# Expert stage of a streaming encoder: stores on another queue, seven key groups taken straight through, float32 gate products, one selection at a time

## The chip, the core and the metric

The program runs on one core of one Trainium2 chip. The metric is the device time of one execution in microseconds, and the number that is compared is the median over several runs.

## The reference, cut to what is computed

One encoder layer runs over 256 prompt tokens and 128 sample tokens of width 2048. The change touches the last but one part of the layer, a product-key retrieval over 128 x 128 = 16384 one-neuron experts (PEER):

```python
def one_block(xt):
    q = (xt @ wq).reshape(blk, PEER_HEADS, 2, PEER_DKEY // 2)
    s = jnp.einsum('thpd,hpnd->thpn', q, keys).astype(jnp.float32)
    sv, si = lax.top_k(s, PEER_TOPK)
    cand = (sv[..., 0, :, None] + sv[..., 1, None, :]).reshape(blk, PEER_HEADS, PEER_TOPK * PEER_TOPK)
    ...
    top_v, top_p = lax.top_k(cand, PEER_TOPK)
    e_idx = jnp.take_along_axis(cidx, top_p, -1).reshape(blk, PEER_HEADS * PEER_TOPK)
    gate = jax.nn.softmax(top_v, -1).reshape(blk, PEER_HEADS * PEER_TOPK)
    act = jax.nn.gelu(jnp.einsum('ted,td->te', u_tab[e_idx], xt).astype(jnp.float32))
    coef = (gate * act).astype(xt.dtype)
    return jnp.einsum('te,ted->td', coef, v_tab[e_idx])
```

Before it come the token mixers, after it a layer norm and a gated embedding product. All weights are float32.

## The kernel before, in words

**Two ways through the experts.** The 128 sample tokens fetch their own experts: 256 gathers of 1 MB each (`fetch_experts`, L1420; 128 rows of `u_rows`, then 128 of `v_rows`), issued on GpSimd (L1426) and each used by one VectorE instruction (L1433 for a dot product, L1440 for a weighted sum into `xg`). The 256 prompt tokens go dense: the first product of all 16384 experts with all tokens, times a gate matrix that is zero where a token did not choose the expert, times the second table. This dense way is cut into 256 units of work on TensorE, each with one weight tile `st` of 1 MB (128x2048 f32) and 48 matmuls of 256 columns: 128 units of the first product (`u_unit`, one per row of keys) and 128 of the second (`v_unit`, 16 key groups of 8 rows times 8 slices of the width).

**A weight tile.** Class `Units` loads it on SP's queue (L104, three buffers), ScalarE rounds each half to a high part `wh` (L118), VectorE or GpSimd subtracts for the low part `wl` (L121), with four buffers each of half a tile. Each matmul triple is high x high, high x low, low x high. `lo_on_pool` says how many of the two halves GpSimd takes: during the first products of a tile with an odd number 2, otherwise 1.

**The order.** It is written by hand. A counter advances by one tick per matmul triple, so a unit has 16 ticks; every 15 ticks a gather step is emitted (`GEVERY`; the instruction that uses a gathered tile follows `LAG` = 3 steps behind, `NGB` = 5 tiles), and other work is a generator that is resumed every so many ticks (`start(..., every)`). In the last query projections the sample tokens' selection (`select_fetched`) runs so; the program then empties the list of generators (`drain_to(0)`) before the first unit.

**The dense gates.** `matrices` is one such generator. For each of the two tiles of 128 prompt tokens it runs `select` (top 16 of 128 twice per head, top 16 of 256 sums, indices and softmax on VectorE) and `turn` (transposes on TensorE into the PSUM tile `pe` and into `eT`), both tiles' selections first, every 7 ticks; then `gates_matrix` for both tiles, every 4 ticks. It goes by steps of 4 tokens, 32 per tile, 16 ticks each. In a step VectorE builds one-hot tiles `AB` (L1405), ScalarE scales the first key's one-hots by the high and the low part of the gates (`H`, eight instructions, L1414), TensorE multiplies them in four float32r matmuls of 256 columns into the single PSUM tile `pg` (twice two), and after each two ScalarE copies the high part to `GB` (L1392) and VectorE adds the low part (L1393). Every 8 steps SP stores `GB` (2 MB) to the DRAM tensor `G_dr` (L1395).

**Between the products.** The GELU of every pair of first products is stored by SP to `act_dr` (L1469), 64 stores of 256 KB. In the second products, at the start of each group, SP loads the next group's gates `G` (1 MB, L1491) and four tiles `t` of `act_dr` (L1536, five buffers); after every second unit `coef` multiplies them on VectorE (L1497) and splits them on ScalarE and VectorE (L255, L256) for the next group.

Of the kernel before, what the change touches and what calls it, by code (L numbers as in the profile page):

```python
# [34 lines left out]
NGB = 5  # L35
LAG = 3
NE = 5
GT = 32
# [47 lines left out]
class Units:  # L86
# [21 lines left out]
    def split(self):  # L108
# [10 lines left out]
        on_pool = self.lo_on_pool if i < self.peer or i % 2 else 1  # L119
# [22 lines left out]
def kernel(ctx: ExitStack, tc: tile.TileContext, io):  # L142
# [58 lines left out]
    peer = [("U", i) for i in range(NKEY)] + [("V", g, d) for g in range(NG) for d in range(8)]  # L201
# [1065 lines left out]
    def scores(hp, q):  # L1267
        yield
        p = ps()
        for t in range(3):  # L1270
            mm(p[:, bl(t)], q[:, bl(t)], keysT[:, hp, :])
        A.copy(q, p[:, :T])
        nc.sync.dma_start(s_dr[hp], q[:, :TD])
        scored.append(q[:, TD:])

    def select(pool, score, e, x):
# [19 lines left out]
        si = al([128, NH, 2, TOPK], F32, "si")  # L1296
        A.copy(si, ix)
        ij = al([128, 2, NS], U32, "ij")
        V.tensor_scalar(ij[:, 0], ixp, 4, None, op0=OP.logical_shift_right)
        V.tensor_scalar(ij[:, 1], ixp, 15, None, op0=OP.bitwise_and)  # L1300
        fj = al([128, 2, NS], F32, "fj")
        A.copy(fj, ij)
        V.tensor_sub(x, tv, tv[:, :, 0:1].to_broadcast([128, NH, TOPK]))
# [6 lines left out]
        n = NS // 2  # L1310
        for i in range(4):
            k, s = i % 2, i // 2
# [5 lines left out]
            V.tensor_mul(o, o, si[:, k * 4:(k + 1) * 4, s, None, :].to_broadcast([128, NH // 2, TOPK, TOPK]))  # L1318
# [19 lines left out]
    drain_to(0)  # L1338
    q = None
    scored.clear()  # L1340
# [6 lines left out]
    w3_ctx, w3a_ctx = ExitStack(), ExitStack()  # L1347
    w3 = w3_ctx.enter_context(tc.tile_pool(name="w3", bufs=1))
    e12 = [w3.tile([128, 2, NS], F32, name=f"e12_{t}") for t in range(2)]
    gw = [w3.tile([128, NH, TOPK], F32, name=f"gw{t}") for t in range(2)]  # L1350
    eTs = [w3.tile([128, 2, 128], F32, name=f"eT{t}") for t in range(2)]
    tg = lambda: w3.tile([128, 2, TD], F32, name=uid("t"), tag="T", bufs=3)
    w3a = w3a_ctx.enter_context(tc.tile_pool(name="w3a", bufs=1))
    qs = [w3a.tile([128, TD], F32, name=f"qs{hp}") for hp in range(HP)]
    for hp in range(HP):
        nc.sync.dma_start(qs[hp], s_dr[hp])
# [6 lines left out]
    def turn(t):  # L1363
        for s in range(2):
            P.transpose(pe[:, t, s], e12[t][:, s], ident)
        p = pg()
        P.transpose(p[:, 0:128], gw[t].rearrange("p a b -> p (a b)"), ident)
        eT = eTs[t]
        A.copy(eT[:, 1], p[:, 0:128])
        ghi = w3.tile([128, 128], FR, name=uid("gh"), tag="gh", bufs=2)  # L1370
        A.copy(ghi, eT[:, 1])
        A.copy(eT[:, 0], ghi.bitcast(F32))
# [312 lines left out]
```

## Time and profile before

| what | us |
| --- | --- |
| median of 3 runs | 4243.83 (4242.4 to 4248.89) |
| the profiled execution | 4236.31 |
| its span, first to last instruction | 4234.5 |
| first units' stretch, U (2187.0 to 3215.7) | 1029 |
| second units' stretch, V (3216.1 to 4084.4) | 868 |

How to read it: busy time of TensorE is time in which a matmul is in flight, and a matmul at the lower clock is in flight longer; so the work done in a stretch is better read from the count of matmuls (48 to a unit) than from the busy share. The granted clock stands beside each stretch, and 1.00 is 2.4 GHz.

### The profile page before, as it was taken

The page shows a single profiled execution, that of the slowest core. Times are in us where ns is not written, and L with a number is a line of the kernel's source. Part 1 is how long each engine was busy: PE and PEld are TensorE (multiplying, and loading weights), DVE is VectorE, ACT ScalarE, POOL GpSimd, SP SyncE. Part 2 cuts the span into 40 slices and gives each one's busy share as a digit, 9 for nine tenths or more (in the row PEclk, how much of TensorE's full clock was granted, in tenths as well). Part 3 has the DMA queues.
Part 4 walks back from the last instruction along what each step waited for, and adds up shares of the span by engine and source line. Part 5 has one row for each costly group of instructions (what it writes and reads, how often), then busy time and mean ns, then how long its engine had stood idle before and what let it go on. Part 6 is the DMA issues. An engine that isn't in the chain of part 4 may idle for free.

```text
span 4234.5 us, 66000 instructions
## 1 busy us (share of the span) xinstructions
PE 3900.6 (92%) x26270; PEld 3821.4 (90%) x26270; DVE 2841.5 (67%) x4293; ACT 1822.4 (43%) x3170; POOL 1594.0 (38%) x1253
## 2 busy tenths in 40 slices
PE   8999999999999999999877788888897989999989
PEld 7999999999999999999877687788897988898989
DVE  5777777754555433344779966666567877888776
ACT  5444555443444423234323266766333333333343
POOL 1122112121211000003325556556775666666572
PEclk9999999999999999999988899999999999999999
DMA  6233333334343534343336777788999999999734
GB/s 232 92 108 117 128 125 107 116 137 149 138 169 119 211 125 158 121 141 125 113 127 260 292 281 306 306 322 305 361 368 342 366 351 362 367 367 370 300 112 147
DMA packets 190711, 925.63 MB, mean 219 GB/s; under 512 B 23874, under 2 KB 68930, under 8 KB 94786
## 3 DMA queue, kind: packets, MB, share of 16 engines
q1 hardware_dynamic: 153106, 652.22, 41.6%
q0 software_dynamic: 36864, 268.45, 16.2%
q8 instruction: 206, 3.38, 0.3%
q14 instruction: 103, 0.84, 0.1%
q10 hardware_dynamic: 432, 0.74, 0.1%
HBM read 848.19 MB, written 73.15 MB: 218 GB/s over the span
## 4 chain that ended last, share of the span: by engine, by line
PE 61%; DVE 15%; DMA 11%; ACT 5%; issue 4%; SPq 2%; POOL 2%; POOLq 0%; ACTq 0%; DVEq 0%
PE ps L173 59%; DMA st<-w_u 6%; DMA st<-w_v 5%; DVE wl L121 3%; DVE gb L1433 2%; ACT wh L118 2%; SPq L1536 2%; POOL wl L121 2%; ACT H L1414 2%; DVE xg L1440 1%; ACT GB L1392 1%; DVE AB L1405 1%; DVE GB L1393 1%; DVE oh L1315 0%; ACT t L252 0%
## 5 line engine op out<-in xcount | busy, mean ns | idle before, releaser
L173 PE MATMUL ps<-k,wh 128*128 128x384 f32 (+2 forms) x5664 | 1484.9, 343 | 5.0 <-DVE k L256 4.4
L121 DVE TENSOR_TENSOR wl<-st,wh 128x1024 fp32r<-128x1024 f32 x608 | 905.7, 1499 | 592.5 <-ACT wh L118 592.1
L118 ACT CAST wh<-st 128x1024 fp32r<-128x1024 f32 x965 | 987.8, 1047 | 559.6 <-PE ps L173 265.9
L121 POOL TENSOR_TENSOR wl<-st,wh 128x1024 fp32r<-128x1024 f32 x357 | 870.7, 2444 | 899.7 <-ACT wh L118 817.3
L173 PEld LDWEIGHTS ps<-k,wh 128*128 128x128 f32 (+1 forms) x5664 | 1004.3, 188 | 15.9 <-DVE k L256 6.1
L173 PE MATMUL ps<-k,wl 128*128 128x384 f32 (+2 forms) x2832 | 957.2, 338 | 3.5 <-POOL wl L121 2.9
L173 PE MATMUL ps<-x,wh 128*128 128x256 f32 x4096 | 776.7, 291 | 22.7 <-ACT wh L118 22.7
L173 PEld LDWEIGHTS ps<-x,wh 128*128 128x128 f32 x4096 | 666.0, 200 | 24.2 <-ACT wh L118 24.1
L173 PE MATMUL ps<-x,wl 128*128 128x256 f32 x2048 | 598.9, 292 | 62.0 <-DVE wl L121 37.2
L173 PE MATMUL ps<-chi,wl 128*128 128x256 f32 x2048 | 597.9, 292 | 51.9 <-POOL wl L121 47.4
L173 PE MATMUL ps<-chi,wh 128*128 128x256 f32 x2048 | 595.2, 291 | 35.5 <-ACT wh L118 35.5
L173 PE MATMUL ps<-clo,wh 128*128 128x256 f32 x2048 | 592.1, 289 | 0.0
L173 PEld LDWEIGHTS ps<-k,wl 128*128 128x128 f32 (+1 forms) x2832 | 530.9, 187 | 5.0 <-POOL wl L121 3.5
L173 PEld LDWEIGHTS ps<-x,wl 128*128 128x128 f32 x2048 | 408.6, 199 | 68.1 <-DVE wl L121 38.9
L173 PEld LDWEIGHTS ps<-chi,wl 128*128 128x128 f32 x2048 | 406.5, 198 | 59.3 <-POOL wl L121 54.4
L173 PEld LDWEIGHTS ps<-chi,wh 128*128 128x128 f32 x2048 | 406.9, 199 | 38.3 <-ACT wh L118 38.2
L173 PEld LDWEIGHTS ps<-clo,wh 128*128 128x128 f32 x2048 | 406.3, 198 | 0.1
L173 PE MATMUL ps<-t,wh 128*128 128x384 f32 (+1 forms) x1536 | 400.6, 342 | 0.0
L1440 DVE SCALAR_TENSOR_TENSOR xg<-gb,gate,xg 128x2048 f32<-128x2048 f32 x128 | 300.4, 2347 | 0.1
L1433 DVE CUSTOM_DVE_ANT_0 gb<-gb,xg 128x2048 f32<-128x2048 f32 x128 | 290.5, 2277 | 10.2 <-DMA gb<-u_rows,idx 10.2
L173 PEld LDWEIGHTS ps<-t,wh 128*128 128x128 f32 x1536 | 280.3, 190 | 0.7
L173 PE MATMUL ps<-t,wl 128*128 128x384 f32 (+1 forms) x768 | 261.0, 340 | 0.2 <-DVE wl L121 0.2
(371 smaller groups left out, 4358.6 us busy)
## 6 DMA issues: line engine op xcount, KB each, us to landing
st<-w_u SPq DMA_DIRECT2D x128, 1024.0 KB, 8.0
st<-w_v SPq DMA_DIRECT2D x128, 1024.0 KB, 9.5
st<-w_gdn SPq DMA_DIRECT2D x64, 1024.0 KB, 6.8
st<-w_ml SPq DMA_DIRECT2D x48, 1024.0 KB, 6.3
st<-w_ga SPq DMA_DIRECT2D x16, 1024.0 KB, 5.2
st<-w_a SPq DMA_DIRECT2D x16, 1024.0 KB, 4.8
st<-w_gb SPq DMA_DIRECT2D x16, 1024.0 KB, 4.7
st<-w_b SPq DMA_DIRECT2D x16, 1024.0 KB, 4.8
```

The source lines that it names most:

```text
L118: self.nc.scalar.copy(hi, src)
L121: eng.tensor_sub(lo, src, hi.bitcast(F32))
L173: P.matmul(out, lhsT, rhs, start=start, stop=stop, skip_group_check=True)
L1392: A.copy(g, v[:, :, 0, :])
L1393: V.tensor_add(g, g, v[:, :, 1, :])
L1405: V.tensor_tensor(AB, iob, pe[:, t, :, c, None].to_broadcast(sh), op=OP.is_equal)
L1414: A.activation(H8[:, k, x], AB[:, 0, k].bitcast(F32), AF.Copy, scale=eT[:, x, 4 * j + k:4 * j + k + 1])
L1433: V.tensor_tensor_reduce(out=b, in0=b, in1=xg, op0=OP.mult, op1=OP.add, scale=1.0, scalar=0.0, accum_out=dots[:, c:c + 1])
L1440: V.scalar_tensor_tensor(xg, b, gate[:, c - NS:c - NS + 1], xg, op0=OP.mult, op1=OP.add)
L1536: nc.sync.dma_start(a, act_dr[g * EG // 2 + j])
```

## The change

1. *Stores leave SP's queue.* The stores of the scores (`s_dr`), of the first products (`act_dr`) and of the gates (`G_dr`) are issued on ScalarE's queue.
2. *Seven key groups go straight through.* The first 72 first products (9 groups, `NS0`) are stored as before. Then come seven rounds of 24 units: 8 first products of group 9 + r, whose pairs go to `coef` from SBUF; 8 second products of stored group r; 8 second products of group 9 + r. The last 16 units are the second products of groups 7 and 8. The stored tiles of the next group are loaded one at a time, after every second unit of the first eight second products.
3. *Gates by float32 products.* ScalarE scales the one-hots in place by the gate itself (four instructions a step instead of eight), TensorE multiplies in four float32 matmuls of 128 columns, and ScalarE copies the whole step at once; VectorE's add is gone. A step has 9 ticks instead of 16.
4. *One tile at a time.* Tile 0 is selected (every 6 ticks), its gates are built (every 3), then tile 1 (every 5, then 3). The one-hot part of `select` goes by quarters instead of halves.
5. *First products start earlier:* while the sample tokens' selection ends, six first products run in place of emptying the list, without gathers; their results go to `act_dr` one by one.
6. *Smaller ones:* GpSimd takes 1 + i % 2 of the halves of all tiles from the first product on, to the end of the program; four gather tiles instead of five.

```diff
-NGB = 5
+NGB = 4
+NS0 = 9
...
-        on_pool = self.lo_on_pool if i < self.peer or i % 2 else 1
+        on_pool = self.lo_on_pool if i < self.peer else 1 + i % 2
...
-        nc.sync.dma_start(s_dr[hp], q[:, :TD])
+        nc.scalar.dma_start(s_dr[hp], q[:, :TD])
...
-    drain_to(0)
+    while tasks or nu % 2:
+        a = t2()[:, :TD]
+        u_unit(a)
+        nc.scalar.dma_start(act_dr[nu // 2][:, nu % 2], a)
+        nu += 1
...
+                    A.copy(GB.rearrange("p n t -> p t n")[:, t0:t0 + 4, :], p.rearrange("p (t n) -> p t n", t=4))
+                    if i % (GT // 4) == GT // 4 - 1:
+                        nc.scalar.dma_start(G_dr[(t * 128 + 4 * i) // GT], GB.rearrange("p n t -> p (n t)"))
                 yield
...
+                if j > 0:
+                    ab = AB[(j - 1) % 2]
+                    for k in range(4):
+                        A.activation(ab[:, 0, k], ab[:, 0, k], AF.Copy, scale=gT[:, 4 * (j - 1) + k:4 * (j - 1) + k + 1])
                 yield
+                if j > 0:
+                    p = pg()
+                    for k in range(4):
+                        mm(p[:, k * 128:(k + 1) * 128], ab[:, 1, k], ab[:, 0, k])
                 yield
...
+    for r in range(NG - NS0):
+        n = NS0 + r
+        Cs[n] = []
         for j in range(EG // 2):
+            a = w4b.tile([128, 2, TD], F32, name=uid("a"), tag="a", bufs=2)
+            for i in range(2):
+                u_unit(a[:, i])
+            Cs[n].append(coef(n, j, a, last_c))
+            if j == 0:
+                load_G(r + 1)
...
         for d in range(8):
+            if d == 0:
+                load_G(n + 1 if n + 1 < NG else last)
+            elif d % 2:
+                got[d // 2] = load_act(r + 1, d // 2)
+            add_values(d, v_unit(r, d, Cs[r]))
...
+        for d in range(8):
+            o = v_unit(n, d, Cs[n])
             if d % 2 == 0:
+                Cs[r + 1].append(coef(r + 1, d // 2, got[d // 2], next_c))
...
+            add_values(d, o)
```

On SP's queue the first products' stretch reads before (`act_dr` is the store of a pair, `st` a weight tile):

```order
L104 DMA st213_21311<-w_u 128x2048
L104 DMA st214_21387<-w_u 128x2048
L1469 DMA act_dr0_21246<-t2421_21310 128x512
L104 DMA st215_21463<-w_u 128x2048
L104 DMA st216_21537<-w_u 128x2048
L1469 DMA act_dr1_21247<-t2431_21462 128x512
```

and after:

```order
L105 DMA st220_21741<-w_u 128x2048
L105 DMA st221_21822<-w_u 128x2048
L105 DMA st222_21901<-w_u 128x2048
L105 DMA st223_21978<-w_u 128x2048
L105 DMA st224_22058<-w_u 128x2048
```

Between two weight tiles' loads no store is left on SP. In the second products SP had, at the turn of a group:

```order
L104 DMA st356_32314<-w_v 128x2048
L1491 DMA G3130_32377<-G_dr_21240 128x8x256
L1536 DMA t3131_32379<-act_dr12_21258 128x512
L1536 DMA t3132_32381<-act_dr13_21259 128x512
L1536 DMA t3133_32383<-act_dr14_21260 128x512
L1536 DMA t3134_32385<-act_dr15_21261 128x512
L104 DMA st357_32387<-w_v 128x2048
```

and has, in a round:

```order
L1482 DMA G2874_27680<-G_dr_21624 128x8x256
L105 DMA st293_27682<-w_v 128x2048
L1487 DMA t2878_27749<-act_dr4_21147 128x512
L105 DMA st294_27751<-w_v 128x2048
L105 DMA st295_27815<-w_v 128x2048
L1487 DMA t2883_27879<-act_dr5_21148 128x512
L105 DMA st296_27881<-w_v 128x2048
```

The four loads of `act_dr` stand apart, each behind two weight tiles. On ScalarE, where the gates are built, one step (and a unit with it) read before:

```order
L1414 ACTIVATE H82783_26560<-AB2780_26522,eT1_21204 128x128 x8
L252 ACTIVATE t2771_26404<-ps2778_26495 128x256
L118 CAST wh276_0_26577<-st276_26489 128x1024
L1392 COPY GB2752_26164<-pg2786_26591 128x2x128
L118 CAST wh276_1_26613<-st276_26489 128x1024
L1392 COPY GB2752_26164<-pg2789_26629 128x2x128
```

and two steps read after:

```order
L1413 COPY GB2528_22931<-pg2544_23154 128x4x128
L119 CAST wh237_1_23180<-st237_23059 128x1024
L1422 ACTIVATE AB2542_23121<-AB2542_23121,gT2520_22839 128x128 x4
L1413 COPY GB2528_22931<-pg2547_23200 128x4x128
L258 ACTIVATE t2537_23058<-ps2543_23147 128x256
L1461 DMA act_dr12_21155<-t2537_23058 128x512
L119 CAST wh238_0_23228<-st238_23141 128x1024
L1422 ACTIVATE AB2545_23168<-AB2545_23168,gT2520_22839 128x128 x4
```

A step has one copy and four scalings, with one or two casts of a weight half among them. Where the rounds begin, ScalarE reads after:

```order
L1415 DMA G_dr_21624<-GB2806_26715 128x4096
L119 CAST wh283_1_27066<-st283_26948 128x1024
L258 ACTIVATE t2822_26947<-ps2828_27039 128x256
L1461 DMA act_dr35_21178<-t2822_26947 128x512
L261 CAST chi2837_27131<-t2833_27122 128x512
L261 CAST chi2839_27136<-t2834_27124 128x512
L261 CAST chi2841_27141<-t2835_27126 128x512
L261 CAST chi2843_27146<-t2836_27128 128x512
L119 CAST wh284_0_27153<-st284_27033 128x1024
```

The last store of gates, and then four splits (`chi`) that need those gates back from DRAM, stand ahead of the next unit's weight cast. Before, some thirty first products lay between that store and the splits.

## Rows read from the trace of the kernel before

**Rows 1.** The page's first part: busy time of each engine, its share of the span and its instructions.

```profile
PE 3900.6 (92%) x26270; PEld 3821.4 (90%) x26270; DVE 2841.5 (67%) x4293; ACT 1822.4 (43%) x3170; POOL 1594.0 (38%) x1253
```

**Rows 2.** The view by stretches of the span: start and end in us, length, then busy us and instructions of PE, PEld, DVE, ACT and POOL, the granted clock, the DMA engines' busy share and GB/s. The stretches are: selection (twice, the second cut to what the view of rows 7 covers), gates, first products after the gates, second products with gathers, second products without, the last group, the products after it.

```profile
2181.00:2441.00 260.00, 177.76 (x1289) 173.28 (x1289) 246.45 (x550) 73.97 (x103) 134.69 (x68) 0.83 0.66 248
2200.00:2440.00 240.00, 164.74 (x1217) 160.79 (x1217) 230.77 (x512) 68.14 (x93) 131.43 (x67) 0.83 0.68 258
2441.00:2951.00 510.00, 423.07 (x3280) 411.74 (x3280) 337.65 (x354) 354.55 (x818) 305.74 (x160) 0.93 0.79 307
3000.00:3150.00 150.00, 141.95 (x1154) 139.81 (x1154) 96.52 (x64) 57.22 (x74) 122.52 (x62) 0.98 0.95 367
3240.00:3940.00 700.00, 635.23 (x5024) 627.08 (x5024) 578.95 (x432) 240.43 (x263) 435.62 (x217) 0.95 0.94 364
4000.00:4035.00 35.00, 35.00 (x294) 35.00 (x294) 17.10 (x14) 14.43 (x19) 18.63 (x9) 1.00 0.49 175
4043.00:4097.00 54.00, 39.05 (x248) 36.29 (x249) 46.06 (x39) 27.28 (x58) 54.00 (x48) 0.87 0.24 82
```

**Rows 3.** TensorE in order of time, in the last group at the upper clock and in the second products at the lower: start and duration in us of single matmuls; seven matmuls lie between the first two rows, three between the others.

```profile
4062.03 0.28 PE L173 MATMUL ps<-clo,wh 128*128 128x256 f32 x1
...
4062.99 0.28 PE L173 MATMUL ps<-chi,wh 128*128 128x256 f32 x1
...
3506.63 0.42 PE L173 MATMUL ps<-chi,wl 128*128 128x256 f32 x1
...
3507.48 0.41 PE L173 MATMUL ps<-chi,wh 128*128 128x256 f32 x1
```

**Rows 4.** The second products' matmuls that use the low half `wl`: count, duration in ns (least, median, most), first and last start in us.

```profile
L173 PE MATMUL ps<-chi,wl x2048: 277/283/583, 3216.1 to 4084.4; 128*128 128x256 f32 x187
```

**Rows 5.** The waits of SP's queue from 2190 to 4085: the waiting line, what it waited for, us in total, times, longest.

```profile
SPq L1469 <- ACT t L252: 834.7, 64, 29.9
SPq L104 <- DVE wl L121: 596.9, 109, 14.1
```

**Rows 6.** The chain of waits that ended last, inside 3200 to 3960, by line; then SP's queue in order of time at the start of one group of second products (start, us, line, count).

```profile
by line: PE ps L173 30.8%; DMA st<-w_v 24.4%; SPq L1536 8.7%; DVE xg L1440 8.4%; issue 8.2%; DVE wl L121 6.5%; POOL wl L121 5.3%; ACT wh L118 1.7%; DVE t L1497 1.2%; POOL gb L1426 1.2%; DVE acc L1528 1.0%; ACT chi L255 0.9%; SPq L1491 0.6%;
...
3478.26 9.47 SPq L1536 DMA_DIRECT2D t<-act_dr  x4
3487.85 44.02 SPq L104 DMA_DIRECT2D st<-w_v  x8
```

**Rows 7.** Two of VectorE's groups from 2200 to 2440, each shape apart: count, busy us, mean ns, idle before; then the gathers of the first table: count, ns (least, median, most), first and last start.

```profile
L1433 DVE CUSTOM_DVE_ANT_0 gb<-gb,xg 128x2048 f32<-128x2048 f32 x25 | 56.8, 2272 | 0.0
L121 DVE TENSOR_TENSOR wl<-st,wh 128x1024 fp32r<-128x1024 f32 x14 | 27.7, 1977 | 0.9 <-ACT wh L118 0.9
...
L1426 POOL DMA_INDIRECT gb<-u_rows,idx x128: 937/960/1885, 2212.3 to 3153.7; - x128
```

**Rows 8.** The gates: the first and the last one-hot tile with their count; then ScalarE's groups from 2441 to 2951; then, from 2460 to 2940, TensorE's gate matmuls with their waits.

```profile
L1405 DVE TENSOR_TENSOR AB<-msk,pe x64: 1197/1215/1249, 2441.0 to 2951.4; 128x1024 fp32r<-128x1024 f32 x64
...
L1414 ACT ACTIVATE H<-AB,eT 128x128 fp32r<-128x128 f32 x504 | 154.3, 390 | 35.0 <-DVE AB L1405 35.0
L118 ACT CAST wh<-st 128x1024 fp32r<-128x1024 f32 x126 | 133.0, 1056 | 66.3 <-DMA st<-w_u 66.3
L1392 ACT COPY GB<-pg 128x256 f32<-128x256 f32 x125 | 79.3, 634 | 54.6 <-PE pg L173 54.6
L252 ACT ACTIVATE t<-ps 128x256 f32<-128x256 f32 x63 | 22.9, 363 | 0.7 <-PE ps L173 0.7
...
L173 PE MATMUL pg<-H,AB 128*128 128x256 f32 x234 | 55.7, 316 | 86.9 <-DVE GB L1393 80.0 <-ACT H L1414 4.6 <-ACT t L252 2.3
```

**Rows 9.** Single rows in order of time (start, us): three plain float32 matmuls of 128x128 (six records) and what follows them on TensorE; eight scalings in a row on ScalarE; the issue of a DMA on ScalarE's queue.

```profile
2176.99 0.94 PE L173 MATMUL ps<-keysT,t 128*128 128x128 f32 x6 [0.46 <-ACT t L252]
2177.68 0.60 PE L173 MATMUL ps<-t,wh 128*128 128x386 f32 x2
...
2810.39 2.46 ACT L1414 ACTIVATE H<-AB,eT 128x128 fp32r<-128x128 f32 x8 [0.84 <-DVE AB L1405]
...
0.73 0.40 ACTq L213 DMA_DIRECT2D pt<-pT  x1
```

**Rows 10.** Groups from 3240 to 3940 on GpSimd, VectorE and ScalarE, each shape apart; below them the low half's subtraction on both engines over the whole span (ns, least, median, most).

```profile
L121 POOL TENSOR_TENSOR wl<-st,wh 128x1024 fp32r<-128x1024 f32 x105 | 254.0, 2419 | 247.0 <-ACT wh L118 246.2
L121 DVE TENSOR_TENSOR wl<-st,wh 128x1024 fp32r<-128x1024 f32 x105 | 190.5, 1815 | 68.3 <-ACT wh L118 68.3
L1426 POOL DMA_INDIRECT gb<-v_rows,idx x112 | 182.4, 1629 | 18.6 <-issue 9.7 <-DVE xg L1440 1.4 <-PE ps L173 1.1
L1497 DVE TENSOR_TENSOR t<-t,G 128x512 f32<-128x512 f32 x52 | 35.4, 681 | 1.7 <-DMA t<-act_dr 1.7
L255 ACT CAST chi<-t 128x512 fp32r<-128x512 f32 x52 | 32.3, 620 | 312.4 <-DVE t L1497 304.1 <-DMA st<-w_v 8.3
...
L121 DVE TENSOR_TENSOR wl<-st,wh x608: 1204/1225/6132, 8.3 to 4216.6; 128x1024 fp32r<-128x1024 f32 x152
L121 POOL TENSOR_TENSOR wl<-st,wh x357: 1845/2422/3498, 26.3 to 4215.7; 128x1024 fp32r<-128x1024 f32 x179
```

**Rows 11.** From issue to landing, us (least, median, most): the stores of `GB` to `G_dr`, and then the loads of `G` from it.

```profile
DMA to landing us min/median/max: 8.9/10.5/13.0
...
DMA to landing us min/median/max: 13.3/14.4/15.4
```

More of the change, by code (lines that the diff above doesn't have):

```diff
@@ L1300, in select @@
         V.tensor_scalar(ij[:, 1], ixp, 15, None, op0=OP.bitwise_and)
+        V.tensor_sub(x, tv, tv[:, :, 0:1].to_broadcast([128, NH, TOPK]))
+        for _ in range(3):
+            yield
+        si = al([128, NH, 2, TOPK], F32, "si")
+        A.copy(si, ix)
         fj = al([128, 2, NS], F32, "fj")
         A.copy(fj, ij)
-        V.tensor_sub(x, tv, tv[:, :, 0:1].to_broadcast([128, NH, TOPK]))
         act(x, x, AF.Exp)
@@ L1309, in select @@
         V.tensor_mul(x, x, sm[:, :, None].to_broadcast([128, NH, TOPK]))
-        n = NS // 2
-        for i in range(4):
-            k, s = i % 2, i // 2
+        n = NS // 4
+        for i in range(8):
+            k, s = i % 4, i // 4
             c = slice(k * n, (k + 1) * n)
@@ L1337, with u_unit @@
         start(scores(hp, q))
-    drain_to(0)
     q = None
+    act_dr = [dram.tile([128, 2, TD], F32, name=f"act_dr{i}") for i in range(NS0 * EG // 2)]
+    def u_unit(a):
+        p = project(x1T, w=TD)
+        act(a, p[:, :TD], AF.Gelu_apprx_tanh)
+    nu = 0
+    while tasks or nu % 2:
[3 more added lines that the diff above has]
+        nu += 1
+    a = None
     scored.clear()
@@ L1361 @@
     pg = lambda: pbank[0].tile([128, 512], F32, name=uid("pg"), tag="pg", bufs=1)
[L1363 to L1372, printed above, removed]
-        V.tensor_sub(eT[:, 1], eT[:, 1], eT[:, 0])
-        yield
@@ L1441, in fetch_experts @@
             yield
-    def matrices():
-        for t in range(2):
-            yield from select(w3a, lambda hp: qs[hp][:, bl(t)], e12[t], gw[t])
-            yield from turn(t)
-        w3a_ctx.close()
-        w3b_ctx = ExitStack()
-        w3b = w3b_ctx.enter_context(tc.tile_pool(name="w3b", bufs=1))
-        pace[0] = 4
-        for t in range(2):
-            yield from gates_matrix(t, w3b)
-        w3b_ctx.close()
-    pace = [7]
+    pace = [6]
     fetches.append([fetch_experts(), clock[0]])
     start(matrices(), every=pace)
-    units.lo_on_pool = 2
-    act_dr = [dram.tile([128, 2, TD], F32, name=f"act_dr{i}") for i in range(NKEY // 2)]
-    def u_unit(a):
-        p = project(x1T, w=TD)
-        act(a, p[:, :TD], AF.Gelu_apprx_tanh)
-    def u_pair(pi, al):
-        a = al()
+    while nu < NS0 * EG:
+        a = tg()
         for i in range(2):
             u_unit(a[:, i])
-        nc.sync.dma_start(act_dr[pi], a)
-    for pi in range(NKEY // 2 - 3):
-        u_pair(pi, tg)
+        nc.scalar.dma_start(act_dr[nu // 2], a)
+        nu += 2
+    a = None
     drain_to(0)
@@ L1581 @@
         z = w5.tile([128, 2, T], F32, name=f"z{d}")
-        o = v_unit(NG - 1, d, Cs[NG - 1])
+        o = v_unit(last, d, Cs[last])
         p = ps()
```

154 lines of the change are left out of this document (74 added, 80 removed).

## The prediction

> **What bounds the kernel now.** I read the busy shares first. TensorE is in flight for 92% of the span [rows 1], so time can only come from stretches where it works below its own pace. That pace I took from single matmuls: eight of 256 columns take 0.96 us at the upper clock, 0.12 each, and four take 0.85 us at the lower, 0.21 each [rows 3]. A unit of 48 matmuls is therefore 5.76 us at best, and the stretch without gathers has it (294 matmuls in 35 us, 5.71 a unit) [rows 2].
>
> Next the stretches, where the reader should divide matmuls by 48 [rows 2, 4]. The 128 second products take 868 us, 6.8 each; with gathers, 5024 matmuls in 700 us are 6.69 a unit. First products after the gates come to 6.24 (1154 in 150 us). While the gates are built a step, with one unit in it, takes 8.1 us (63 intervals in 510 us) [rows 8]. The selection takes 260 us for some 27 units, 9.6 each, and there VectorE is busy 96% of the time [rows 2]. So the 256 units, which at full pace would take 1475 us, take from 2181 to 4084.
>
> Then the waits. SP stands 835 us for the GELU whose result it is to store, 64 times and up to 30 us [rows 5], and the loads of weight tiles are queued behind. In the second products one of four loads of `act_dr` waits for a buffer, 9.5 us for the four once a group, and the weights come late behind it: the chain there has 24% on `st<-w_v` and 9% on SP's L1536 [rows 6]. In the gates TensorE waits 80 of 480 us for VectorE's add to free `pg` [rows 8]. A stall costs twice: the granted clock is 0.83 in the selection, 0.93 to 0.95 in the gates and second products, and 1.00 where nothing stalls [rows 2].
>
> **The change part by part.** Up to 2181 only the stores of scores move, beside full work on TensorE: nothing, against 16 issues of 0.4 us on ScalarE [rows 9] if they showed, 6 us.
>
> *Six units without gathers.* They run while VectorE ends the first selection, some 30 us, up to the first gather at 2212 [rows 7]. I take 5.9 each and 5 us for SP, whose reloads of scores wait for the sixth result: **40 us** (35 to 50).
>
> *Two selections, 40 steps each by 6 and by 5 ticks, 440 ticks, 27.5 units.* They stay bound by VectorE. From its 230.8 us [rows 2] I take off gathers' uses and low halves (56.8 and 27.7) [rows 7] and 12 for the sample tokens' selection, which the first gather awaits until 2212: 134 for both. The new stretch adds 29 uses of 2.27 us and 13.75 low halves of 1.98: 134 + 66 + 27 = 227, at 96% busy 236, with the two reloads of scores **240 us** (227 to 275; the quarters shorten single instructions, not their sum). Four gather tiles make GpSimd wait for the use one step back instead of two; no row has that wait, and the nearest, 15 ticks of slack against 2.3 us of use, says nothing; up to 10 us lie in the upper end.
>
> *Gates, 64 steps of 9 ticks.* TensorE has 27 matmuls of 0.12 and four float32 ones of 0.23 each (three take 0.69) [rows 9]: 4.16 us. ScalarE has one copy of 128x512. No row has it; the bounds are the contiguous cast of that size, 0.62 [rows 10], and two of today's strided copies, 1.27 [rows 8]; I take 1.1, near the strided ones. Four scalings are half of 2.46, 1.23 [rows 9], and 9/16 of a unit's two casts and GELU [rows 8] 1.4, issues 0.2: 3.9 in all. But they form a loop on the one `pg`: matmuls 0.92, copy 1.1, scaling 1.23, a cast between them on average 0.9, four handovers of some 0.1: **4.6 us a step**. The least is TensorE's 4.16; the most is today's loss per step (8.1 less a unit of 6.2, 1.9) on top of 4.16, 6.1. With four steps that have no matmuls: 64 x 4.6 + 13 = **307 us** for 38 units (279 to 403). Today 64 units and the same gates take 510.
>
> *The turn.* The last gates go to DRAM and straight back, and ScalarE has the splits ahead of the next weight cast. Landing of the store 10.5, of the load 14.4 [rows 11], four rounds of multiply, cast and subtract some 7, cast and low half 3.5, less the 8.7 us of units that TensorE still has: 27, at the lower clock for a moment after it: **30 us** (15 to 40).
>
> *Seven rounds, 168 units.* A unit moves 1.05 MB of weights, 16/15 of a gather, and 1/24 of two `G` and four `t`: 2.30 MB, against 2.43 in today's second products. It is what a first product moves today, whose stores weigh as much, and GpSimd has the same 1.5 halves; these run at 6.24 with the stores still on SP [rows 2]. For less speaks that the stores are off SP and no group begins with a blocked queue. For more: a load of `G` that waits for the last `coef`, with a weight tile behind it, once a round, and eight casts `chi` a round that hold ScalarE until VectorE has multiplied (304 us for 52 today, in the shade of TensorE for the most part) [rows 10]. I take 6.2: **1042 us** (5.9 to 6.69, 991 to 1124).
>
> The Trainium skill bears on the stores (DMA: Bandwidth & Descriptors, "Issuing engines are not separate DMA queues"): all DMAs run on the same 16 engines, and issuing from several only saves the sequencer's time. By it the rounds would keep today's rate and gain by bytes alone, 6.69 x 2.30/2.43 = 6.33, 22 us more than I take. The rows speak for a bit more, as what SP lost was not issue time but waiting for another engine's result.
>
> *Last 16 units* at 6.0, with 5 us for the last gathered rows, which end only just ahead of the last group: 101. There GpSimd is busy without a gap for 54 us [rows 2], and four more low halves of 2.42 us [rows 10] fall to it: 10. **111 us** (100 to 120). *The rest* is as today, **150 us**; GpSimd takes 8 halves more there, with 32 of 125 us busy [rows 2]; if they showed, 8 us.
>
> Sum: 2181 + 40 + 240 + 307 + 30 + 1042 + 111 + 150 = 4101. Today the same stretches are 2181 + 260 + 510 + 265 + 868 + 150 = 4234. The profiled execution lies 1.8 us above its span, and the median of the runs 7.5 us above that execution: 4101 + 1.8 + 7.5 = **4110 us**, 3.2% less. Most of it comes from the gates (64 units with them took 510; 38 with them 307 and 26 without 161) and from the second products (0.5 us a unit).
>
> **The rivals.**
>
> *The second products' loss stays.* What they lose today is not SP's blocked loads but the DMA engines' load (0.94 busy) and the casts that wait for VectorE; then the rounds run at 6.69 and the last group of gathers too: 4110 + 82 + 4 = 4196. For it: the chain has 24% on transfers of `w_v` even while SP is free. Against it: first products at the same 0.95 run at 6.24.
>
> *The gate loop is no better.* A step costs 6.1, as ScalarE waits on TensorE and TensorE on ScalarE in turn: 64 x 1.5 = 96 more, 4206. For it: today's waits are of this kind. Against: VectorE's add, which ended 80 of 87 us of them, is gone.
>
> *Better than that.* Weights are always early: gates at TensorE's 4.2 and rounds at 5.95: 26 + 42 less, 4042. The DMA engines then carry 2.30 MB in 5.95 us, 387 GB/s, against 367 in the fastest stretch [rows 2].
>
> *Slower: GpSimd becomes the bound.* In the rounds it has 1.5 halves of 2.42 and 16/15 of a gather's 1.63 [rows 10], 5.4 us a unit beside 5.76 of TensorE. Its subtraction has taken up to 3.5 us, and VectorE's 1.8 on average beside it where 1.2 is the least [rows 10]. If the halves slow to 3.5 a unit takes 7.0, and the 184 units of rounds and last groups 0.8 more each: 4257. It decides against the change from 6.92 a unit on (133/184 = 0.72 above 6.2), a mean half of 3.45. Against it: the same 1.5 halves run beside first products today at 6.24, though without adds and splits on VectorE. VectorE's one-hot tiles, with one input in PSUM, never took over 1.25 us beside the same GpSimd [rows 8], and its low halves, with both inputs in SBUF, up to 6.1 [rows 10]. The Trainium skill (SBUF, "The single rule") has a mechanism for this: a VectorE instruction with two inputs in SBUF and a GpSimd one that reads SBUF exclude each other for their whole length. The rows agree. By that rule more halves on GpSimd and fewer on VectorE leave the overlap much as it is, so it does not raise the chance of this case.
>
> **How the numbers follow.** The forecast, 4060 to 4165, has 0.55; the second products' loss 0.13; the gate loop 0.10; better 0.14; GpSimd 0.08, of which 0.03 end at or near today's time. The range runs from 4042 less a little, 4035, to past 4206, 4210. It leaves out GpSimd and the ends of better, under 0.2. A measurement of this kernel can tell 0.2%, some 8 us, from no change. Every case but GpSimd's lies over 30 us below today's time: faster 0.91, within 0.2% 0.03, slower 0.06.
>
> **What would show it.** Right: SP no longer waits for ScalarE's GELU; the matmuls of the rounds come to 6.1 to 6.3 us a unit; scaled tiles of the gates follow each other by 4.4 to 5 us; a gap of TensorE of 25 to 30 us where the rounds begin, with ScalarE's `chi` waiting; VectorE over 90% busy in both selections; GpSimd without a gap in the last group. Wrong: TensorE waiting for GpSimd's `wl` more than for ScalarE's `wh` in the rounds; a step of the gates over 5.5 us; a clock under 0.93 in the rounds.

## The result, and the profile after

| | before | changed kernel |
| --- | --- | --- |
| median, us | 4245.60 (4242.4 to 4248.89, 4 runs) | 4127.48 (4124.06 to 4131.58, 4 runs) |
| ratio | | 0.9722 (95% interval 0.9705 to 0.9739) |
| span of the profiled execution | 4234.5 | 4121.9 |

The change takes 2.8% off. The prediction was 4110 with a range of 4035 to 4210.

The page's busy time of TensorE after, which stands against the 92% of [rows 1]:

```profile
PE 3888.2 (94%) x26526; PEld 3814.7 (93%) x26526; DVE 2741.1 (67%) x4127; ACT 1753.3 (43%) x2848; POOL 1729.1 (42%) x1325
```

The stretches of the changed kernel (from:to, length, then busy time with counts of PE, PEld, DVE, ACT, POOL, the granted clock, the DMA share and GB/s), against [rows 2]: first selection, first gates, second selection, second gates, the turn, 144 units of the rounds, then the last group of gathers and what follows it:

```profile
2236.00:2357.00 121.00, 95.87 (x734) 94.20 (x734) 116.70 (x263) 38.61 (x51) 71.53 (x38) 0.90 0.77 285
2357.00:2500.00 143.00, 140.17 (x1162) 138.31 (x1162) 99.08 (x99) 111.35 (x215) 91.31 (x49) 1.00 0.94 355
2500.00:2627.00 127.00, 81.29 (x592) 79.55 (x591) 113.14 (x248) 33.55 (x44) 61.38 (x33) 0.83 0.68 252
2627.00:2757.00 130.00, 127.72 (x1064) 126.32 (x1063) 90.16 (x78) 103.57 (x201) 84.21 (x45) 1.00 0.90 350
2757.00:2805.00 48.00, 28.82 (x216) 28.11 (x215) 18.60 (x20) 17.10 (x28) 19.07 (x10) 0.79 0.87 321
2840.00:3739.00 899.00, 848.75 (x6910) 837.98 (x6909) 672.12 (x481) 334.57 (x385) 727.67 (x371) 0.98 0.95 370
...
3890.00:3966.00 76.00, 57.98 (x420) 56.19 (x418) 46.18 (x40) 33.76 (x67) 63.31 (x50) 0.87 0.35 124
3966.00:4121.00 155.00, 142.69 (x782) 137.45 (x780) 115.41 (x115) 58.05 (x93) 67.88 (x32) 0.99 0.37 128
```

In the gates TensorE is in flight for 98% of the time at the upper of its two clock levels, 2.4 GHz, where it had waits and a granted clock of 0.93 before [rows 2]. The selections are the new hole: VectorE is busy 96% and 89% of them, TensorE 79% and 64%. The rounds run at 0.98.

What SP waits for between 2190 and 4000 (total, times, longest), against [rows 5]:

```profile
SPq L105 <- POOL wl L122: 802.1, 129, 14.9
SPq L105 <- DVE wl L122: 597.3, 110, 19.8
SPq L1482 <- DVE a L1493: 86.3, 7, 13.0
```

The 835 us behind ScalarE's GELU are gone. SP now waits where a load queue should, at its own line (L105) for a weight buffer to come free; the largest of the new waits is the load of `G` behind `coef`, seven times.

The landmarks of the changed kernel, one-hot tiles and second and first products, each with durations (ns: least, median, most) and its first and last start:

```profile
L1407 DVE TENSOR_TENSOR AB<-msk,pe x64: 1206/1220/1223, 2357.0 to 2756.2; 128x1024 f32<-128x1024 f32 x64
L174 PE MATMUL ps<-chi,wl x2048: 276/283/583, 2840.5 to 3965.7; 128*128 128x256 f32 x187
L174 PE MATMUL ps<-x,wl x2048: 277/281/582, 2178.9 to 3739.7; 128*128 128x256 f32 x187
```

Below, "the rounds" are the 144 units from the first second product to the last first product, 48 first and 96 second products: here 3739.7 - 2840.5 = 899 us, 6.24 each.

The turn, on TensorE, ScalarE and SP in the timeline (start, length, instruction, in brackets the idle time before it and what ended it), one fence for each:

```profile
2793.60 0.80 PE L174 MATMUL ps<-x,wh 128*128 128x256 f32 x2 [16.85 <-ACT wh L119]
```

```profile
2786.05 0.62 ACT L261 CAST chi<-t 128x512 fp32r<-128x512 f32 x1 [14.51 <-DVE t L1493]
```

```profile
2774.45 1.01 SPq L1482 DMA_DIRECT2D G<-G_dr  x2
2775.51 4.53 SPq L1487 DMA_DIRECT2D t<-act_dr  x4
2780.14 0.89 SPq L105 DMA_DIRECT2D st<-w_u  x2
```

The gates' way to DRAM and back holds ScalarE at `chi` for 14.5 us with the weight cast behind it. SP asks for the two weight tiles behind two `G` and four `t`, some 6 us late.

### The profile page after: what moved, and what is told of

The parts are those of the page before. It is cut to its first block, busy times and chain, and to the rows that moved or that the text cites. A ratio compares the mean times of both kernels' runs of the same rounds, so it can differ in the third digit from the quotient of the medians.

```text
span 4121.9 us, 65955 instructions
## 1 busy us (share of the span) xinstructions
PE 3888.2 (94%) x26526; PEld 3814.7 (93%) x26526; DVE 2741.1 (67%) x4127; ACT 1753.3 (43%) x2848; POOL 1729.1 (42%) x1325
## 4 chain that ended last, share of the span: by engine, by line
PE 70%; DVE 12%; issue 5%; DMA 4%; POOL 4%; ACT 3%; SPq 0%; ACTq 0%; POOLq 0%; DVEq 0%
PE ps L174 68%; POOL wl L122 3%; DMA st<-w_u 2%; DVE wl L122 2%; DMA st<-w_v 2%; PE pg L174 1%; DVE gb L1444 1%; ACT wh L119 1%; POOL gb L1437 1%; DVE oh L1323 1%; DVE oh L1326 1%; DVE z L349 0%; DVE z L348 0%; DVE xg L1451 0%; DVE cd L1298 0%
## 5 line engine op out<-in xcount | busy, mean ns | idle before, releaser
L122 POOL TENSOR_TENSOR wl<-st,wh 128x1024 fp32r<-128x1024 f32 x429 | 1046.3, 2449 | 624.4 <-ACT wh L119 545.9
L122 DVE TENSOR_TENSOR wl<-st,wh 128x1024 fp32r<-128x1024 f32 x536 | 771.5, 1450 | 539.0 <-ACT wh L119 534.6
L174 PE MATMUL ps<-x,wh 128*128 128x256 f32 x4096 | 759.2, 287 | 28.8 <-ACT wh L119 28.3
L174 PEld LDWEIGHTS ps<-x,wh 128*128 128x128 f32 x4096 | 647.8, 194 | 30.1 <-ACT wh L119 29.3
L174 PEld LDWEIGHTS ps<-x,wl 128*128 128x128 f32 x2048 | 397.6, 194 | 102.2 <-DVE wl L122 72.4
```

The source lines that it names most:

```text
L122: eng.tensor_sub(lo, src, hi.bitcast(F32))
L174: P.matmul(out, lhsT, rhs, start=start, stop=stop, skip_group_check=True)
```

## The experiments

A ratio is that to the kernel before, timed on the same chip, with its 95% interval. "Changed" stands for the kernel after, ratio 0.9722. Where two kernels are compared "by the ratios", their two ratios are; "by the medians" the times may come from two chips.

**Stores alone.** The kernel before, with its three kinds of stores issued on ScalarE.

```diff
-        nc.sync.dma_start(act_dr[pi], a)
+        nc.scalar.dma_start(act_dr[pi], a)
```

(and so for `s_dr` and `G_dr`)

> The kernel before, with the three kinds of stores (scores, first products, gates) issued on ScalarE's queue and nothing else changed. Theory (the queue): SP no longer waits 835 us for the GELU, weight tiles are asked for about one unit earlier, and the first products' stretch of 1029 us loses part of its 83 us of casts waiting for weights in the gates; 4220, at least 10 us below 4244, and the stretch of second products unchanged at 6.69 us a unit. Rival (same 16 DMA engines): SP's wait cost nothing, as the loads landed in time or were limited by the engines; within 8 us of 4244.

4174.04, ratio 0.986 (0.9844 to 0.9877): 63 us by the medians, more than the theory asked for. The stretch after the gates, in the windows view:

```profile
2920.00:3100.00 180.00, 179.00 (x1522) 178.60 (x1523) 119.34 (x85) 74.45 (x96) 158.37 (x81) 1.00 1.01 410
```

First products run at 5.68 us a unit instead of 6.24, at TensorE's own pace, with the DMA engines at a share of 1.01. All of the gain lies before the second products, which take 868 us as before. The landmarks, one-hot tiles and first products:

```profile
L1405 DVE TENSOR_TENSOR AB<-msk,pe x64: 1193/1214/1255, 2440.4 to 2913.2; 128x1024 fp32r<-128x1024 f32 x64
L173 PE MATMUL ps<-x,wl x2048: 276/280/582, 2183.2 to 3150.2; 128*128 128x256 f32 x187
```

The gates take 473 us instead of 510 and the first products behind them 237 instead of 264.

**Spaced loads alone.** The kernel before, with the next group's four `act_dr` loads issued one per two units.

```diff
+            if d in (1, 3, 5):
+                nxt[(d + 1) // 2] = load_act(g + 1, (d + 1) // 2)
+            elif d == 7 and g + 2 < NG:
+                nxt[0] = load_act(g + 2, 0)
```

> The kernel before, with the loads of stored first products issued one at a time, one after every second unit, a unit ahead of their use, in place of four at the start of a group. Theory (SP blocked by a full set of buffers at the start of a group, weights late behind it): second products with gathers go from 6.69 to about 6.3 us a unit, 4195 in all, and SP's 9.5 us at the start of a group is gone. Rival (DMA engines 0.94 busy, and casts that wait for VectorE): still 6.6 to 6.7, 4235 to 4250.

4187.46, ratio 0.989 (0.9873 to 0.9906): 50 us, all in the second products, 814 us instead of 868. The stretch of [rows 2] from 3240 to 3940:

```profile
3240.00:3940.00 700.00, 665.02 (x5400) 656.41 (x5401) 627.30 (x464) 253.28 (x280) 468.56 (x229) 0.99 0.98 387
```

5400 matmuls instead of 5024, 6.22 a unit. The prediction's rival, that the rate stays at 6.69, falls here: about half of what the second products lose against 5.76 was SP's wait for a buffer. The other half stays, and no run removes it; TensorE's own waits there are now nearly all for GpSimd's low half, 29.5 of 34.8 us.

**Float32 gates alone**, in the kernel before, at 9 ticks a step, stores still on SP.

```diff
-        pace[0] = 4
+        pace[0] = 3
...
+                    A.activation(ab[:, 0, k], ab[:, 0, k], AF.Copy, scale=gT[:, 4 * (j - 1) + k:4 * (j - 1) + k + 1])
...
+                    mm(p[:, k * 128:(k + 1) * 128], ab[:, 1, k], ab[:, 0, k])
```

> The kernel before, with the gates by plain float32 products and steps of 9 ticks; both selections still first, stores still on SP. Theory (the loop through VectorE's add is what the gates lost): 4.3 us a step, so 288 us for 38 units and 28 more units at 6.24, 463 in place of 510: 4195. Rival (the steps are quick in the changed kernel only because weights come early there): 5 us a step or more, 4235 or above.

4224.78, ratio 0.9972 (0.9957 to 0.9987): 13 us. The theory fell; the step is the rival's, the time lies between them.

```profile
L1379 DVE TENSOR_TENSOR AB<-msk,pe x64: 1207/1220/1224, 2439.3 to 2761.2; 128x1024 f32<-128x1024 f32 x64
```

63 intervals in 321.9 us are 5.1 a step, 0.9 more than the 4.2 of the changed kernel. The time that the shorter step frees is filled with first products that are still starved (2555 matmuls in the 350 us after it, 6.58 a unit); the last of them starts at 3201.1:

```profile
L173 PE MATMUL ps<-x,wl x2048: 276/281/582, 2183.2 to 3201.1; 128*128 128x256 f32 x187
```

**All three on the kernel before**, without straight rounds, selections as before.

> The kernel before, with stores on ScalarE's queue, the loads of stored products spaced, and the gates by float32 products in 9 ticks: all three edits together, and no group taken straight through. Theory (late weights hold the new gates back, so that the three edits add up to more than 63 + 50 + 13 = 126 us below 4237): gate steps at 4.3 instead of 5.1, 4070 to 4090, below the changed kernel. Rival (the straight rounds carry gain of their own, by 15 MB less and no stores): 4110 or above.

4078.7, ratio 0.9616 (0.9588 to 0.9644): 163 us, more than 63 + 50 + 13 = 126, and 45 below the changed kernel by the ratios, 49 by the medians, as the theory had it. Its one-hot tiles and first products, and in the windows view plain first and second products:

```profile
L1379 DVE TENSOR_TENSOR AB<-msk,pe x64: 1206/1221/1224, 2442.0 to 2719.7; 128x1024 f32<-128x1024 f32 x64
L173 PE MATMUL ps<-x,wl x2048: 276/281/583, 2184.7 to 3109.9; 128*128 128x256 f32 x187
```

```profile
2740.00:3050.00 310.00, 310.00 (x2615) 310.00 (x2614) 197.88 (x144) 128.10 (x164) 272.37 (x141) 1.00 1.01 409
3110.00:3810.00 700.00, 665.60 (x5372) 656.82 (x5371) 620.85 (x463) 254.91 (x282) 472.43 (x232) 0.98 0.98 387
```

The gates need the stores off the queue to come down to 4.4 us a step: they take 278 us instead of 322, and the first products behind them 390 instead of 440. So beside the float32 gates moving the stores is worth 44 + 50 = 94 us, beside the old gates it was 38 + 27 = 65. This accounts for 29 of the 37 by which the whole exceeds its parts, and most of it lies not in the gates but in the plain first products, of which shorter gates leave more, each starved as long as the stores are on SP. Plain units run at 5.69 and 6.25; 48 of one and 96 of the other would take 873 us, where the rounds take 899.

**Stores back on SP**, in the changed kernel.

> The changed kernel, with the three kinds of stores back on SP's queue. Theory (with stores on SP, weight tiles are asked for late, which cost the kernel before 63 us in its 128 first products): only the 72 stored first products are hit, selections and gates; gate steps go from 4.2 to about 5 us (64 x 0.8 = 51) and the rest by a few us: 4165 to 4180. Rival (what made the stores dear in the kernel before was the old gate loop): within 15 us of the changed kernel, 4120 to 4140.

4170.51, ratio 0.9834 (0.9805 to 0.9863): 43 us more than changed, the theory's side. The wait is back, a step of the gates takes 4.9 us, and all of the loss lies before the rounds (`AB` from 2361.4 to 2803.8, first second product at 2890.0, rounds 899):

```profile
SPq L1461 <- ACT t L258: 438.8, 32, 24.4
```

**GpSimd one half of every tile**, in the changed kernel.

```diff
-        on_pool = self.lo_on_pool if i < self.peer else 1 + i % 2
+        on_pool = self.lo_on_pool if i < self.peer else 1
```

> The changed kernel, with GpSimd taking one half of every weight tile from the first product on, in place of 1 and 2 in turn. Theory (VectorE bounds the selections, GpSimd the last group): selections lose 14 halves of 2 us, 27, and the last group gains 10; rounds stay at 6.25; 4144. Rival (GpSimd at over 80% holds the rounds back): rounds at 6.15 or less, 17 us and more, so 4127 or below.

4102.55, ratio 0.9686 (0.967 to 0.9702): 15 us below changed by the ratios, 25 by the medians. My theory fell: the selections take 6 us longer and not 27. The rounds take 888, 11 less, 6.17 a unit (landmarks, then the windows view):

```profile
L174 PE MATMUL ps<-chi,wl x2048: 278/283/582, 2844.4 to 3951.6; 128*128 128x256 f32 x187
L174 PE MATMUL ps<-x,wl x2048: 276/281/583, 2180.5 to 3732.8; 128*128 128x256 f32 x187
```

```profile
2845.00:3730.00 885.00, 845.45 (x6882) 836.81 (x6881) 741.13 (x551) 332.34 (x384) 590.11 (x297) 0.98 0.96 374
```

VectorE takes 70 us more and GpSimd 138 less than in the changed kernel's window. The time is the rival's, but not its reason as it stands: TensorE waits for GpSimd's low half as long in these rounds (30.5 us) as in the changed kernel's (31.3). The last units and what follows them gain 14: there, in the changed kernel, TensorE waits for GpSimd's low half (waits from 3890 to 3966; the other rows of this view are left out):

```profile
PE ps L174 <- POOL wl L122: 17.3, 6, 7.7
```

**First group's coefficients after each pair**, in the changed kernel, so that the gates' way back is hidden by eight first products.

```diff
-    Cs[0] = [coef(0, j, got[j], next_c) for j in range(EG // 2)]
+    Cs[0] = []
...
+            if r == 0:
+                Cs[0].append(coef(0, j, got[j], next_c))
```

> The changed kernel, with the four coefficients of group 0 made one after each pair of the first round's first products, instead of all four ahead of them. Theory (TensorE's gap of 17 us at the turn is ScalarE held by casts that wait for gates on their way through DRAM): one more pair lies between, the gap shrinks to a few us: 4108, 10 to 15 us less than the changed kernel's 4120 to 4127. Rival (the weight tiles behind SP's loads of gates are late anyway): within 5 us.

4126.93, ratio 0.9729 (0.97 to 0.9758): nothing, as the rival said. The cast no longer waits for VectorE, but for the tile that SP asked for behind six loads (ScalarE in the timeline):

```profile
2797.91 1.99 ACT L119 CAST wh<-st 128x1024 fp32r<-128x1024 f32 x2 [15.68 <-DMA st<-w_u]
```

TensorE's gap is 11.6 us here instead of 16.9, and the rounds take 902.

**`G` asked for later**, in the changed kernel at the group's fifth second product, when its `coef` is long done.

```diff
-            if d == 0:
+            if d == 4:
```

> The changed kernel, with the load of the next group's gates (the buffer that the last coefficients of the round free) issued at the fifth second product of a round instead of ahead of the first. Theory (SP waits there for VectorE's last multiplication, 13 us at most, with a weight tile queued behind, and TensorE stalls some 7 us once a round): rounds from 6.24 to about 5.95 us a unit, 40 us less, 4080 to 4090. Rival (DMA engines 0.95 busy at 370 GB/s bound the rounds): 6.2 or more, 4115 or above.

4118.54, ratio 0.9705 (0.9674 to 0.9736): 9 us by the medians, and the interval also holds no change against the changed kernel. In the rounds SP's wait at this line falls from 74.6 to 0.7 us, and the rounds from 899 to 896: SP had that time to spare. The number is the rival's; its reason, the DMA engines as the bound, isn't shown, as they carry 371 GB/s here and carried 410 in the first run.

**These three together** in the changed kernel.

> The changed kernel with three edits together: one half of every weight tile on GpSimd (alone 17 to 25 us), the load of the next group's gates at the fifth second product (alone about 6), and the first round's coefficients one after each pair (alone nothing). Theory (the rounds are held by GpSimd's halves and by the gates' load, one showing only when the other is gone): rounds below 6.05 us a unit, 4075 to 4090. Rival (the edits add up): 4095 to 4105, rounds at 6.12 or more.

4106.15, ratio 0.9694 (0.9673 to 0.9714): no better than the halves alone, and a little over the rival's 4105. The rounds take 886.5, the rival's side; the turn still has its gap:

```profile
2800.63 0.79 PE L174 MATMUL ps<-x,wh 128*128 128x256 f32 x2 [14.01 <-ACT wh L119]
```

**Both halves on GpSimd while selecting**, in the changed kernel.

```diff
-        on_pool = self.lo_on_pool if i < self.peer else 1 + i % 2
+        on_pool = self.lo_on_pool if i < self.peer else 2 if self.sel else 1 + i % 2
```

> The changed kernel with both halves of every weight tile on GpSimd during the two selections. Theory (VectorE bounds them): 121 and 127 us shrink by 10 each, 4100 to 4108. Rival (as VectorE's instructions get slower beside GpSimd's): within 6 us of the changed kernel, 4118 to 4130.

4107.69, ratio 0.9697 (0.9676 to 0.9717): 11 us below changed by the ratios, 20 by the medians. The time is what the theory said, the way to it only in part. The one-hot tiles, and of them the last of the first gates and the first of the second, in the changed kernel and then here:

```profile
L1410 DVE TENSOR_TENSOR AB<-msk,pe x64: 1206/1221/1224, 2363.1 to 2751.4; 128x1024 f32<-128x1024 f32 x64
```

```profile
2489.41 1.22 DVE L1407 TENSOR_TENSOR AB<-msk,pe 128x1024 f32<-128x1024 f32 x1
2626.91 1.21 DVE L1407 TENSOR_TENSOR AB<-msk,pe 128x1024 f32<-128x1024 f32 x1
```

```profile
2497.51 1.22 DVE L1410 TENSOR_TENSOR AB<-msk,pe 128x1024 f32<-128x1024 f32 x1
2618.81 1.22 DVE L1410 TENSOR_TENSOR AB<-msk,pe 128x1024 f32<-128x1024 f32 x1
```

The second selection is 16 us shorter (121.3 instead of 137.5 between these tiles), the first 3 longer (from the first gather, 2239.3). The gates take 5 more, and the first second product, at 2835.0, comes 5.5 us earlier than in the changed kernel. Another 10 come in the rounds, 889, which the edit does not touch. So a rate of the rounds between 886 and 902 is not read as the mark of one edit alone.

**The same on the kernel before with three edits.**

> The kernel before with the three edits of the earlier run (4079) and, while the dense tiles are selected, both halves of every weight tile on GpSimd. Theory (VectorE bounds the selections, 96% busy): it sheds 13 halves of 2 us, the selections' 258 us shrink to 235, 4055 to 4065 in all. Rival (halves on GpSimd slow VectorE's other instructions by what VectorE saves, as one half on GpSimd cost the changed kernel's selections nothing): within 8 us of 4079.

4067.6, ratio 0.9603 (0.9582 to 0.9623), the fastest of all, 11 us below the kernel without it by the medians, 6 by the ratios, whose intervals overlap; the time lies between the two expectations. The selections end at 2428.7 instead of 2442.0. Landmarks, then plain units in the windows view:

```profile
L1380 DVE TENSOR_TENSOR AB<-msk,pe x64: 1206/1221/1223, 2428.7 to 2707.1; 128x1024 f32<-128x1024 f32 x64
L174 PE MATMUL ps<-chi,wl x2048: 277/283/582, 3093.9 to 3913.0; 128*128 128x256 f32 x187
```

```profile
2740.00:3050.00 310.00, 310.00 (x2642) 309.98 (x2642) 204.20 (x147) 127.52 (x164) 277.86 (x142) 1.00 1.01 412
3100.00:3800.00 700.00, 661.17 (x5370) 652.51 (x5369) 624.03 (x464) 253.75 (x280) 471.11 (x232) 0.99 0.98 388
```

**The changed kernel with all that helped**, and SP's loads of the turn behind the first pair's weight tiles:

```diff
-    load_G(0)
-    load_G(NS0)
-    got = [load_act(0, j) for j in range(EG // 2)]
...
+            if r == 0 and j == 0:
+                load_G(NS0)
+                load_G(0)
+                got = [load_act(0, k) for k in range(EG // 2)]
```

> The changed kernel with five edits: one half of every weight tile on GpSimd instead of one or two in turn, both halves there while the dense tiles are selected, the group's G load at its fifth second product, the first group's coefficients cast after each pair, and SyncE's loads of gates and of the turn's activation tiles behind the first pair's weight tiles. Theory (the changed kernel's loss against the kernel before with three edits is its halves, its selections and its turn, and the straight rounds themselves cost nothing): 20 us for the halves, 20 for the selections and some 15 for the turn off 4127, so 4060 to 4072, at or under the 4068 of the kernel without rounds, with TensorE's longest wait at the turn under 5 us and rounds of 6.15 us a unit or less. Rival (the rounds lose by themselves, since each adds GpSimd's gather and its load of gates beside two kinds of product): 4085 or above, whatever the turn does.

4079.74, ratio 0.9634 (0.961 to 0.9658): 37 us below changed by the ratios, between the two expectations. The landmarks and the turn's longest gap:

```profile
L175 PE MATMUL ps<-chi,wl x2048: 277/283/582, 2818.5 to 3927.2; 128*128 128x256 f32 x187
...
L175 PE MATMUL ps<-x,wl x2048: 276/281/583, 2179.0 to 3707.9; 128*128 128x256 f32 x187
```

```profile
2773.53 0.50 PE L175 MATMUL ps<-x,wh 128*128 128x256 f32 x2 [3.57 <-ACT wh L120]
```

The turn is mended: from the last one-hot tile to the first second product it takes 73.7 us, where the run with the three edits took 83.3 and the changed kernel 84.3. The rounds still take 889. Against the fastest kernel (its span 4062.2, second products from 3093.9 to 3913.0) I compare at equal work. There a plain first product takes 5.63 us (2642 matmuls in 310) and a second one 6.26 (5370 in 700). With 80 first products done: 2818.5 here, 3093.9 less 48 x 5.63 = 2824 there. The 144 units: 889 against 48 x 5.63 + 96 x 6.26 = 871. The last 32 second products: 219 against 819 - 601 = 218. The rest: 150 against 149. So of the 15 us between the two spans the rounds lose 18, and the front wins 5 back. The intervals of the two ratios overlap by 0.0013, so that a gain of over some 5 us by the whole restructuring is out. That the rounds cost something rests on single traces: 886 to 889 in the three with one half a tile on GpSimd, 871 and 873 for the same units in the two without rounds. No run adds the rounds alone to the kernel before; four gather tiles, the six early units and one tile at a time weren't tried one by one either.

## Why the prediction was right, by its own steps

The bound was read rightly: TensorE below its pace, because SP's queue stood for other engines' results. The sum came to 4101, the span to 4121.9. That it is only 21 us short is in part luck: the gates' 34 us hide more than half of the 56 by which the other terms together were too small. By its terms:

| term | predicted | measured | off by |
| --- | --- | --- | --- |
| six units without gathers, to | 2221 | 2236 | +15 |
| two selections | 240 | 121 + 127 = 248 | +8 |
| gates | 307 | 143 + 130 = 273 | -34 |
| turn and units to the last 32 | 30 + 152 x 6.2 = 972 | 2757 to 3740 = 983 | +11 |
| last 32 second products | 99 + 111 = 210 | 3740 to 3966 = 226 | +16 |
| the rest | 150 | 156 | +6 |

*Six units.* Mis-sized: the reload of scores was taken at 5 us. VectorE's first look at the dense scores waits 9.4 us for `qs<-s_dr`, and TensorE stands 9.3 us for a low half of VectorE's just before, which the sum didn't have:

```profile
2226.39 0.58 PE L174 MATMUL ps<-x,wl 128*128 128x256 f32 x1 [9.33 <-DVE wl L122]
```

```profile
2235.72 0.29 DVE L1267 MAX8 sv<-qs 128x8 f32<-128x128 f32 x1 [9.38 <-DMA qs<-s_dr]
```

*Selections.* Right in size, and in the bound for the second: taking low halves off VectorE shortened the selections by 13 us on the kernel before with three edits, and on the changed one the second by 16, but not the first. The wait that four gather tiles were feared to bring is there, GpSimd stands 48 us in the two selections for the use of a tile, but TensorE waits only 6 for GpSimd's halves in them.

*Gates.* The step that failed most. I let a serial loop on the one `pg` set the step, 4.6 us. The 31 intervals of tile 0 take 132.4 us, 4.27 each, those of tile 1 4.17, against the 4.16 that I had named as TensorE's least. The new copy took 1.14 us (1.1 taken) and four scalings 1.27 (1.23), so the durations were right; what was wrong is that the loop's pieces stand in line. They overlap, as one turn of the loop shows (copy, scaling, matmuls, next copy; the rows between are left out):

```profile
2689.31 1.15 ACT L1413 COPY GB<-pg 128x512 f32<-128x512 f32 x1
2690.20 1.29 ACT L1422 ACTIVATE AB<-AB,gT 128x128 f32<-128x128 f32 x4
2690.68 1.36 PE L174 MATMUL pg<-AB 128*128 128x128 f32 x8 [0.16 <-ACT AB L1422]
2692.30 1.14 ACT L1413 COPY GB<-pg 128x512 f32<-128x512 f32 x1
```

The matmuls start 0.48 us after the first of four scalings, and the turn takes 3.0 us from copy to copy with a weight cast in it (at 2691.37). That is below TensorE's 4.16, so that TensorE sets the step, with first products between the gates' matmuls. The rival of a step at 6.1 is out.

*Turn.* The mechanism is right (ScalarE at `chi`, weight casts behind it), the size too large: a gap of 16.9 instead of 27. A second cause lay ready behind it, unnamed: SP's weight tiles behind its loads of gates. That is why removing the first left a gap of 11.6 and the time as it was, and removing both took the gap to 3.6.

*Rounds.* 6.24 against 6.2 is right in number and wrong in reason. I took the 6.24 of plain first products as what 2.30 MB a unit costs. With the stores off SP those same first products run at 5.68, at 410 GB/s. So 6.24 was a starved rate, and the agreement is luck: the 26 us that the rounds lose over a plain mix (899 against 873) were hidden in my yardstick. What I expected of fewer bytes did not come: the rounds move less than second products (2.30 MB against 2.43) and take 6.16 at best where the plain mix takes 6.06.

*Where the gain came from.* I put most of it to the gates and to the second products, by the straight rounds. By the runs on the kernel before, stores alone bring 63, spaced loads 50 and the gates 13, together 163; the straight rounds aren't needed for any of it. The prediction weighed the rule of the Trainium skill that issuing DMAs from several engines only saves the sequencer's time (DMA: Bandwidth & Descriptors, "Issuing engines are not separate DMA queues"). Here changing the engine that issues, and nothing else, was worth 63 us, since a store at the head of SP's queue held the loads behind it for up to 30 us [rows 5]. The measurement decides: the saving is the queue's waits, not its issue time.

*GpSimd.* Not the bound, as forecast: the kernel stays far below 4257. But one of the prediction's signs of being wrong did come, TensorE waiting for GpSimd's `wl` more than for ScalarE's `wh` in the rounds (2840 to 3740):

```profile
PE ps L174 <- POOL wl L122: 31.3, 31, 1.8
PE ps L174 <- ACT wh L119: 14.4, 4, 4.8
PE ps L174 <- DVE wl L122: 3.9, 2, 2.0
```

It was a poor sign: the second products of the kernel before show the same order, 31.8 and 28.5 us in 700, and the wait for GpSimd stays at 30.5 with one half a tile. Its halves weren't free, though: the prediction's 10 us for the last group and up to 8 behind it are where 14 us come back with one half a tile, 7 in each. Of the 16 us that the last 32 units took too long this leaves 9 open.

*Signs.* Two of the six signs of being right came: SP's wait for the GELU is gone, and the rounds run at 6.24. A step of the gates took 4.2 us and not 4.4 to 5, the gap was shorter, VectorE was 89% busy in the second selection, and GpSimd had gaps of up to 5.5 us in the last group.

**What stays open.** Why the rounds' units run at 6.16 to 6.27 us. TensorE's own waits above are 50 of the 899 us; the fastest kernel's second products have 38 in 700, nearly all for GpSimd (31.9), and its plain first products none. In the changed kernel's chain over the rounds 16% is transfers of weight tiles and 8% GpSimd's low half. More `chi` casts per second product cannot be it, as the plain second products have the same. Open, too, is what halves on GpSimd cost the rounds: 886 to 889 us in three traces with one half a tile, 889 to 902 in five with one and two in turn. Five gather tiles in the rounds weren't tried.

## What to carry to other kernels

Keep stores whose data comes late off the queue that prefetches weights, and look for loads in it that wait for a buffer: those two small edits alone brought 63 and 50 us. Before a rate is used as a yardstick for a new stage, ask whether the old stage was itself starved. Try each part of a large change on the old kernel too: here the simple parts without the restructuring gave 4079 (4068 with one more edit), the whole change 4127.

## What was not expected of the hardware

The DMA engines of one core carried 409 to 412 GB/s over 180 to 310 us (weights, gathers and stores) with TensorE in flight for all but 1 us of them at 2.4 GHz; the fastest stretch before showed 367 [rows 2]. Savings did not add: 63 + 50 + 13 became 163 on the kernel before. On the changed one 15, 0 and 7 (by the ratios) became 12, which their intervals don't tell from a plain sum.
